# A static scheduler's clock, its arena's choice of holes, and the priority of staging subtractions, in a one-core transformer step

## The chip, the core and the metric

The kernel runs on one core of one Trainium2 chip. The metric is the device time of one execution in microseconds; before the change three runs took 2660.2, 2662.82 and 2666.45 us, median 2662.82. A core has five engines that each work off a queue of their own in order and meet at semaphores: TensorE (PE, matmuls and transposes into PSUM), VectorE (DVE), ScalarE (ACT), GpSimd (POOL), and SyncE (SP), which here issues the DMAs.

## The reference

One step of an encoder with two layers over 512 prompt and 32 sample tokens, D = 1024, all in float32. Layer 0 mixes tokens with a chunkwise retention, layer 1 with a differential attention against keys and values projected once after layer 0.

```python
def run_trunk(x, c, pos, ...):
    for l in range(2):
        mod = (silu(c) @ w_ada[l] + b_ada[l]).reshape(b, 9, D)
        h = modulate(x, g_norm[l, 0], mod[:, 0], mod[:, 1])        # rms_norm * (1 + scale) + shift
        x = x + 0.5 * mod[:, 2] * rms_norm(swiglu(h, w_ffn_in[l, 0], w_ffn_out[l, 0]), g_norm[l, 1])
        h = modulate(x, g_norm[l, 2], mod[:, 3], mod[:, 4])
        y = retention_mixer(h, ...) if l == 0 else diff_mixer(h, k, v, k_past, v_past, ...)
        x = x + mod[:, 5] * rms_norm(y, g_norm[l, 3])
        h = modulate(x, g_norm[l, 4], mod[:, 6], mod[:, 7])
        x = x + 0.5 * mod[:, 8] * rms_norm(swiglu(h, w_ffn_in[l, 1], w_ffn_out[l, 1]), g_norm[l, 5])
        if l == 0:
            k, v = shared_kv(x, c, ...)
    return x, new_ret, k, v

def diff_attention(q, k, v, lam):          # per head: two softmaxes, o = (p1 - lam * p2) @ v
    p = softmax(where(visible, q @ k.T * DH**-0.5, -inf))
    return (p[:, :, 0] - lam * p[:, :, 1]) @ v
```

## The kernel before

**Layout.** Activations lie with features on the partitions and tokens in the free dimension. The 544 tokens are two halves: H0 has 256, H1 has 288 (256 prompt and the 32 sample tokens). Each half goes through the stages by itself, and the two are interleaved, so that one half's products cover the other's norms.

**Main products.** A weight matrix is cut into units of 128 output features with 8 (some 6) blocks of 128 inputs. Each float32 weight and each operand is split in two parts, a rounded one (fp32r) and what the rounding left, and a block costs three matmuls (hi x hi, hi x lo, lo x hi; L595). There are 17,280 of them, 8,640 for each half; I number them in their order on PE. A weight block comes by DMA into one of three buffers, ScalarE casts it into the high part of a tile `w` (L574), and VectorE subtracts that from the raw weights for the low part (L577): this is *staging*, 544 times, in `w_conv`. There are four `w` tiles, and PE may begin a unit only when both parts are there (`launch`).

**Boundaries.** At the end of a stage, half by half: square the outputs and add them up (L803, L806 on ScalarE, L808 on VectorE), sum over the partitions by matmul (L700), mean and eps (L704), the power -1/2 on GpSimd (L706), broadcast by matmul (L711), scale and add to X (L845, L849); then the same for the norm ahead of the next stage (a second L808, L700, L704, L706, L711), and its operands (L738 on VectorE, L747 on ScalarE, L753 on VectorE). So a half passes L700 and L711 twice at a boundary, and VectorE works between for a chain of 23 rows or more.

**Attention** (`at_head`, `at_block`, `at_sample`). Per head and half two blocks of 128 queries: logits (L1513), mask, maximum, exponentials, the mix of the two softmaxes (L1522 to L1542), transposes (L1548), the product with v (L1555), a norm (L1570 to L1576), transposes (L1584). The 32 sample tokens go in four passes of two heads each (L1622 to L1690). The second half's sixteen blocks and four passes must all be through before the first unit of the output projection (`w_out_b`) of that half, which begins at product 15,048.

**What sets the order.** The whole program is unrolled by a scheduler, `Sched`, that runs when the kernel is built: generators stand for processes, each step names an engine, a cost in ns, a function that records the instructions, and a priority (lower goes first). The scheduler keeps a clock. When an engine is free by that clock, it takes the ready step of the lowest priority number and records it. What comes out is a fixed order on each engine; on the chip every engine keeps to it. The order of main products by unit is fixed beforehand (`plan`, from the path `_path`); where everything else stands among them is what the clock decides. The costs of steps:

```python
def c_r(n):                       # one matmul of a main product with n columns
    return max(256, n) / 2.4 + 3
def c_dve(n):
    return (64 + n) / 0.96
```

**Memory.** Operands lie in tiles `SLOT`, taken in pairs (high and low part); all else of varying size (outputs Y, scores, heads' keys and values, tables) comes from one `Arena`, whose requests wait until a hole is large enough: those of 600 numbers and more take the first hole from the low end, smaller ones the first from the high end. A head of the second half takes 1504 numbers, a block up to 1424, the sample passes 2992 together.

Of the kernel before, what the change touches and what calls it, by code (L numbers as in the profile page):

```python
# [50 lines left out]
def _path():  # L51
# [3 lines left out]
    for e in ((0, 1), (0, 2), "kv", (1, 0)):  # L55
# [10 lines left out]
       0, Q, 0), (F2, 10, Q, 0), (F2, 36, OB, 0), (F2, 47, OB, 0), (F2, 49, F2, 0), (F2, 68, F2, 0)]  # L66
NSLOT = (35, 34)
NW = 4
# [20 lines left out]
class Arena:  # L89
# [3 lines left out]

    def take(self, n):
        hs = self.holes
        for i in (range(len(hs)) if n >= 600 else range(len(hs) - 1, -1, -1)):
            o, m = hs[i]
            if m >= n:
                if m == n:
                    del hs[i]  # L100
                elif n >= 600:
                    hs[i] = (o + n, m - n)
                else:
                    hs[i] = (o, m - n)
                    o += m - n
                return (o, n)
        return None

# [133 lines left out]
def c_r(n):  # L242
    return max(256, n) / 2.4 + 3

# [77 lines left out]
def yoco_step(ctx: ExitStack, tc: tile.TileContext, I, O):  # L322
    nc = tc.nc
# [38 lines left out]
    def fa(r, n=None, o=0, p0=0, p1=P):  # L362
        n = r[1] - o if n is None else n
        return FA[p0:p1, r[0] + o:r[0] + o + n]
# [326 lines left out]
    def rstd(acc, H, dim, pr=0):  # L691

        nb, n = (3, 96) if H else (2, P)
# [3 lines left out]
        def sums():  # L697
            for j in range(nb):
                for g in range(0, n, 32):
# [5 lines left out]
                                                     ALU.mult, ALU.add), pr)  # L705
        yield ("POOL", 200 + 170 * nb, lambda: nc.gpsimd.tensor_tensor(  # L706
            fa(t, nb, 4, 0, n), fa(t, nb, 0, 0, n), NHALF[:n, :nb], ALU.pow), pr)
# [387 lines left out]
    def ret_head(h, oo):  # L1095
# [11 lines left out]
        def finish(b, H, c0, n):  # L1107

            blks = ((0, P), (P, P)) if n == 256 else ((0, n),)
            rows = blks[0][1]  # L1110
            nb = len(blks)
            og = yield from get(2 * n)
            tk = yield from get(256 * nb)
            m = yield from get(8)

            def sq():
                for i in range(nb):
# [4 lines left out]
                                                          ALU.mult, ALU.add))  # L1122
            yield ("POOL", 200 + 170 * nb, lambda: nc.gpsimd.tensor_tensor(
                fa(m, nb, 4, 0, rows), fa(m, nb, 2, 0, rows), NHALF[:rows, :nb], ALU.pow))
# [149 lines left out]
        o = yield from get(256)  # L1274
# [294 lines left out]
    def sub_ln(b, rows, o, m, t):  # L1569
# [3 lines left out]
                                                     ALU.mult, ALU.add))  # L1573
        yield ("POOL", 370, lambda: nc.gpsimd.tensor_tensor(fa(m, 1, 2, 0, rows), fa(m, 1, 1, 0, rows),
                                                            NHALF[:rows, :1], ALU.pow))
# [209 lines left out]
TANH = (1,)  # L1785
FIN_P = 25
CONV_P = 3
# [4 lines left out]
ADA_LEAD = -22  # L1792
ARENA_N = 20344
RETH = 9
# [115 lines left out]
```

## Time and profile before

| | |
|---|---|
| three runs, median | 2662.82 us (2660.2 to 2666.45) |
| the profiled execution, its own time | 2668.01 us |
| its span, first to last instruction | 2666.2 us |
| mean granted TensorE clock | 0.977 |
| main products L595, busy | 2279.6 us, x17280 |
| staging casts L574 (ScalarE), busy | 556.8 us, x544, 1023 ns mean |
| staging subtractions L577 (VectorE), busy | 649.1 us, x544, 1195 ns mean |
| DMA | 400.57 MB, mean 150 GB/s |
| attention logits L1513, busy | 43.7 us, x128 |

Busy times are unions of an engine's intervals. Matmuls are pipelined: a matmul's own duration (292 ns mean for L595) is longer than the distance from one to the next, so a rate is read from how many there are in a stretch without waits. PEclk is the share of full clock that PE was granted; it takes the values 1.00 and 0.50 in the records, and a mean between them is a mix in time. A wait is idle time of an engine before an instruction, put down to what released it.

### The profile page before, as it was taken

The page shows a single profiled execution, that of the slowest core. Times are in us where ns is not written, and L with a number is a line of the kernel's source. Part 1 is how long each engine was busy: PE and PEld are TensorE (multiplying, and loading weights), DVE is VectorE, ACT ScalarE, POOL GpSimd, SP SyncE. Part 2 cuts the span into 40 slices and gives each one's busy share as a digit, 9 for nine tenths or more (in the row PEclk, how much of TensorE's full clock was granted, in tenths as well). Part 3 has the DMA queues.
Part 4 walks back from the last instruction along what each step waited for, and adds up shares of the span by engine and source line. Part 5 has one row for each costly group of instructions (what it writes and reads, how often), then busy time and mean ns, then how long its engine had stood idle before and what let it go on. Part 6 is the DMA issues. An engine that isn't in the chain of part 4 may idle for free. (4 is left out here: it accounts for less than half of the span.)

```text
span 2666.2 us, 48255 instructions
## 1 busy us (share of the span) xinstructions
PE 2558.3 (96%) x19908; PEld 2409.8 (90%) x19908; DVE 1402.8 (53%) x2716; ACT 1040.3 (39%) x2055; POOL 65.3 (2%) x88
## 2 busy tenths in 40 slices
PE   7999999999999999999999999999997999789998
PEld 5899998899999987999997999998897898479997
DVE  5223337754334474223359644557867766457555
ACT  3222224443323343222234424445654544344433
POOL 0000000000000000000000000000100000000000
PEclk9999999999999999999999999999998999789999
DMA  8722325732222258223238735556643454235553
GB/s 332 261 88 88 96 86 171 249 119 93 79 95 75 79 200 306 88 88 96 88 92 306 222 101 155 176 169 235 229 162 109 135 195 155 72 119 165 167 166 106
DMA packets 119549, 400.57 MB, mean 150 GB/s; under 512 B 13344, under 2 KB 31904, under 8 KB 109088
## 3 DMA queue, kind: packets, MB, share of 16 engines
q1 hardware_dynamic: 119328, 397.48, 45.0%
q8 instruction: 156, 2.56, 0.4%
q14 instruction: 65, 0.53, 0.1%
HBM read 384.19 MB, written 13.24 MB: 149 GB/s over the span
## 5 line engine op out<-in xcount | busy, mean ns | idle before, releaser
L595 PE MATMUL ps<-r,w 128*128 128x288 f32 (+1 forms) x17280 | 2279.6, 292 | 22.8 <-DVE w L577 18.2
L595 PEld LDWEIGHTS ps<-r,w 128*128 128x128 f32 x17280 | 2215.1, 192 | 86.3 <-issue 50.6
L577 DVE TENSOR_TENSOR w<-FA,w 128x1024 fp32r<-128x1024 f32 (+1 forms) x544 | 649.1, 1195 | 601.0 <-ACT w L574 599.3
L574 ACT CAST w<-FA 128x1024 fp32r<-128x1024 f32 (+1 forms) x544 | 556.8, 1023 | 958.1 <-PE ps L595 866.6
L931 DVE TENSOR_TENSOR FA<-ps,FA 128x256 f32<-128x256 f32 (+1 forms) x88 | 38.7, 441 | 186.1 <-PE ps L595 181.5
L895 ACT CAST r<-FA 128x256 fp32r<-128x256 f32 (+1 forms) x176 | 73.2, 417 | 129.5 <-DVE FA L931 92.4
L884 DVE TENSOR_TENSOR FA<-ps,FA 128x288 f32<-128x288 f32 (+1 forms) x144 | 63.2, 440 | 103.3 <-PE ps L595 101.2
L747 ACT ACTIVATE r<-FA,MOD 128x256 fp32r<-128x256 f32 (+1 forms) x168 | 63.5, 437 | 73.2 <-DVE FA L738 72.7
L896 DVE TENSOR_TENSOR r<-FA,r 128x256 fp32r<-128x256 f32 (+1 forms) x176 | 76.8, 437 | 23.2 <-ACT r L895 23.2
L501 PE MATMUL ps<-FA,SC 128*32 128x512 f32 x576 | 77.8, 619 | 6.5 <-DMA FA<-in_ada 6.5
L808 DVE TENSOR_TENSOR FA<-FA 128x256 f32<-128x256 f32 (+1 forms) x168 | 73.3, 437 | 13.3 <-ACT FA L806 12.1
L706 POOL TENSOR_TENSOR FA<-FA,NHALF 128x2 f32<-128x2 f32 (+1 forms) x24 | 27.6, 1151 | 1818.9 <-DVE FA L704 1321.2
L928 DVE SCALAR_TENSOR_TENSOR FA<-ps,FA 128x256 f32<-128x256 f32 (+1 forms) x88 | 38.6, 440 | 55.8 <-PE ps L595 55.8
L738 DVE SCALAR_TENSOR_TENSOR FA<-X,DRV,ps 128x256 f32<-128x256 f32 (+1 forms) x168 | 57.7, 397 | 17.2 <-PE ps L711 14.4
L753 DVE SCALAR_TENSOR_TENSOR r<-FA,MOD,r 128x256 fp32r<-128x256 f32 (+1 forms) x168 | 59.0, 402 | 8.9 <-ACT r L747 8.8
L919 ACT ACTIVATE FA<-ps 128x256 f32<-128x256 f32 (+1 forms) x88 | 34.5, 394 | 70.3 <-PE ps L595 70.2
L990 DVE TENSOR_TENSOR FA<-ps,FA 64x256 f32<-64x256 f32 (+1 forms) x128 | 56.1, 438 | 2.0
L986 DVE TENSOR_TENSOR FA<-ps,FA 128x256 f32<-128x256 f32 (+1 forms) x64 | 28.0, 438 | 51.5 <-PE ps L595 51.3
L845 DVE SCALAR_TENSOR_TENSOR FA<-FA,DRV,ps 128x256 f32<-128x256 f32 (+1 forms) x144 | 50.0, 398 | 5.8 <-PE ps L711 5.6
L882 ACT COPY FA<-ps 128x288 f32<-128x288 f32 (+1 forms) x96 | 36.5, 381 | 40.0 <-PE ps L595 40.0
L806 ACT ACTIVATE FA<-FA 128x256 f32<-128x256 f32 (+1 forms) x84 | 35.7, 428 | 31.7 <-DVE FA L884 31.2
L1513 PE MATMUL ps<-FA 128*128 128x128 f32 (+3 forms) x128 | 43.7, 469 | 1.7 <-ACT FA L1496 0.9
(145 smaller groups left out, 1134.1 us busy)
## 6 DMA issues: line engine op xcount, KB each, us to landing
FA<-in_w_ffn_in SPq DMA_DIRECT2D x256, 512.0 KB, 3.3
FA<-in_ada SPq DMA_DIRECT2D x80, 1024.0 KB, 6.7
FA<-in_w_ffn_out SPq DMA_DIRECT2D x95, 512.0 KB, 3.5
FA<-in_w_in_a SPq DMA_DIRECT2D x60, 512.0 KB, 3.3
FA<-in_w_ffn_out SPq DMA_DIRECT2D x61, 384.0 KB, 3.2
FA<-in_w_kv SPq DMA_DIRECT2D x22, 512.0 KB, 5.2
FA<-in_w_out_a SPq DMA_DIRECT2D x19, 512.0 KB, 3.4
FA<-in_w_q_b SPq DMA_DIRECT2D x16, 512.0 KB, 4.3
```

The costliest lines, as they stand in the source:

```text
L501: te.matmul(PS[b][32 * g:32 * g + 32, :], lhsT=SC[:, k, :], rhs=fa(ada_buf[u, k], 512, g * 512), start=(k == 0), stop=(k == 7))
L574: yield act(n, lambda: nc.scalar.copy(hi, src))
L577: yield dve(n, lambda: nc.vector.tensor_tensor(lo, src, hi.bitcast(F32), ALU.subtract))
L595: te.matmul(PS[b][:, :n], lhsT=w[:, a, k, :], rhs=x, start=(k == 0 and j == 0), stop=(k == u.nk - 1 and j == 2))
L738: nc.vector.scalar_tensor_tensor(fa(z, c1 - c0, o), X[:, f, c0:c1], DRV[:, gi, f, s:s + 1], PS[Rb][:, o:o + c1 - c0], ALU.mult, ALU.mult)
L747: nc.scalar.activation(op.hi(H, c0, c1), fa(z, c1 - c0, o), AF.Identity, bias=MOD[:, mi, f, s:s + 1])
L753: nc.vector.scalar_tensor_tensor(op.lo(H, c0, c1), fa(z, c1 - c0, o), MOD[:, mi, f, s:s + 1], op.hi(H, c0, c1).bitcast(F32), ALU.add, ALU. ...
L808: yield dve(n, lambda: nc.vector.tensor_tensor(acc, acc, fa(t), ALU.add))
L884: yield dvp(n, lambda: nc.vector.tensor_tensor(Y[:, f, c], PS[b][:, :n], Y[:, f, c], ALU.add), 15)
L895: yield act(n, lambda: nc.scalar.copy(op.hi(H), src), pr)
L896: yield dve(n, lambda: nc.vector.tensor_tensor(op.lo(H), src, op.hi(H).bitcast(F32), ALU.subtract), pr)
L990: nc.vector.tensor_tensor(fa(t1, n, n, x, x + 64), PS[b][y:y + 64, :n], fa(rr, n, NTOK + c.start, y, y + 64), ALU.mult)
```

## The change

The diff adds two lines near the top, so that line numbers of the changed kernel are higher by two (L595 becomes L597).

```diff
-NSLOT = (35, 34)
+NSLOT = (34, 34)
...
     def take(self, n):
+
         hs = self.holes
-        for i in (range(len(hs)) if n >= 600 else range(len(hs) - 1, -1, -1)):
-            o, m = hs[i]
-            if m >= n:
-                if m == n:
-                    del hs[i]
-                elif n >= 600:
-                    hs[i] = (o + n, m - n)
-                else:
-                    hs[i] = (o, m - n)
-                    o += m - n
-                return (o, n)
-        return None
+        fit = [(m, i) for i, (o, m) in enumerate(hs) if m >= n]
+        if not fit:
+            return None
+        m, i = min(fit)
+        o = hs[i][0]
...
 def c_r(n):
-    return max(256, n) / 2.4 + 3
+    return max(256, n) / 2.4 + 13.3
...
-        yield ("POOL", 200 + 170 * nb, lambda: nc.gpsimd.tensor_tensor(
+        yield ("POOL", 380 + 160 * nb, lambda: nc.gpsimd.tensor_tensor(
             fa(t, nb, 4, 0, n), fa(t, nb, 0, 0, n), NHALF[:n, :nb], ALU.pow), pr)
...
-        yield ("POOL", 370, lambda: nc.gpsimd.tensor_tensor(fa(m, 1, 2, 0, rows), fa(m, 1, 1, 0, rows),
+        yield ("POOL", 540, lambda: nc.gpsimd.tensor_tensor(fa(m, 1, 2, 0, rows), fa(m, 1, 1, 0, rows),
...
-FIN_P = 25
+FIN_P = 0
...
-ARENA_N = 20344
+ARENA_N = 20600
```

`c_r` is the cost by which the scheduler's clock counts a main product's matmul: 109.7 ns becomes 120.0 for 256 columns, 123.0 becomes 133.3 for 288. The `POOL` costs are those of the powers. `FIN_P` is the priority of the staging subtraction among VectorE's ready steps; the norm chain has priorities from 0 to 2, evictions 15 to 20. The arena takes the smallest hole that fits. One tile of `SLOT` goes (256 numbers per partition), and the arena gets 256. No instruction is added or taken away on the compute engines; they are recorded in another order.

The order on PE, at the end of the second half's attention, before the change. The first row is main product 15,084, the others stand directly behind it; `ps_...` are PSUM banks, FA is the arena:

```order
L595 MATMUL ps_150<-r_28_136,w_144 128x288
L1555 MATMUL ps_152<-FA 128x128 x3
L1548 MATMUL ps_154<-CT,FA 128x128 x4
L1555 MATMUL ps_154<-FA 128x128 x4
L1584 MATMUL ps_153<-CT,FA 128x128 x2
L1513 MATMUL ps_152<-FA 128x384
L1513 MATMUL ps_154<-FA 128x384
L1622 MATMUL ps_153<-FA 64x512 x2
L1548 MATMUL ps_152<-CT,FA 128x128 x3
L1555 MATMUL ps_152<-FA 128x128 x3
```

Twenty-four rows of this kind follow each other there without a main product between them, and twenty-one more behind product 15,102. The order after, behind main product 14,864, with the same kinds of rows (L1550 is L1548 before, L1586 is L1584, L1664 is L1662, L1557 is L1555, L1515 is L1513):

```order
L597 MATMUL ps_148<-r_24_97,w_144 128x256
L597 MATMUL ps_148<-r_26_99,w_144 128x256
L597 MATMUL ps_148<-r_27_100,w_144 128x256
L597 MATMUL ps_148<-r_26_99,w_144 128x256
L1550 MATMUL ps_153<-CT,FA 128x128 x3
L597 MATMUL ps_148<-r_2_75,w_144 128x256
L597 MATMUL ps_148<-r_3_76,w_144 128x256
L597 MATMUL ps_148<-r_2_75,w_144 128x256
```

The pieces of attention stand earlier and have main products between them: the last of them now stands behind product 14,928, before behind 15,102. The first L1622 of the sample passes stands behind product 14,214 (L1624), before behind 14,421.

The order on VectorE, at the boundary between attention and the last FFN for the first half, before the change: the operands of the next stage (L738, L753) and three staging subtractions (L577) behind them:

```order
L738 SCALAR_TENSOR_TENSOR FA<-X,DRV,ps_153 128x256 x4
L753 SCALAR_TENSOR_TENSOR r_16_89<-FA,MOD,r_15_88 128x256
L753 SCALAR_TENSOR_TENSOR r_18_91<-FA,MOD,r_17_90 128x256
L753 SCALAR_TENSOR_TENSOR r_0_73<-FA,MOD,r_28_101 128x256
L753 SCALAR_TENSOR_TENSOR r_2_75<-FA,MOD,r_1_74 128x256
L738 SCALAR_TENSOR_TENSOR FA<-X,DRV,ps_153 128x256
L884 TENSOR_TENSOR FA<-ps_147,FA 128x288
L577 TENSOR_TENSOR w_144<-FA,w_144 128x768
L753 SCALAR_TENSOR_TENSOR r_4_77<-FA,MOD,r_3_76 128x256
L577 TENSOR_TENSOR w_142<-FA,w_142 128x768
L577 TENSOR_TENSOR w_143<-FA,w_143 128x768
```

After the change the first two of these three subtractions (the 388th and the 389th of the program, now L579) stand in the first part of the same boundary, between the rows of the norm (L847, L851, L810 are L845, L849, L808 before), ahead of its second sum of squares:

```order
L579 TENSOR_TENSOR w_144<-FA,w_144 128x768
L810 TENSOR_TENSOR FA<-FA 128x256
L847 SCALAR_TENSOR_TENSOR FA<-FA,DRV,ps_152 128x256 x2
L851 TENSOR_TENSOR X<-X,FA 128x256 x2
L847 SCALAR_TENSOR_TENSOR FA<-FA,DRV,ps_152 128x256
L810 TENSOR_TENSOR FA<-FA 128x256
L851 TENSOR_TENSOR X<-X,FA 128x256
L579 TENSOR_TENSOR w_142<-FA,w_142 128x768
L810 TENSOR_TENSOR FA<-FA 128x256
L918 SCALAR_TENSOR_TENSOR FA<-FA,ps_147 128x288
```

The subtractions moved from behind the operands to between the norm's rows. The same holds at the other boundaries: between a half's two rows L700 there stand more subtractions on VectorE, and on PE more main products of the other half. Behind which main product these pairs of L700 rows stand:

| boundary (the half that ends) | before: first, second | after: first, second | subtractions between, before and after |
|---|---|---|---|
| layer 0, FFN to retention, H0 | 3042, 3114 | 3042, 3147 | 1, 6 |
| same, H1 | 3198, 3264 | 3219, 3333 | 1, 5 |
| retention to second FFN, H0 | 6132, 6192 | 6132, 6240 | 1, 5 |
| second FFN to keys and values, H0 | 9276, 9336 | 9276, 9381 | 1, 6 |
| same, H1 | 9432, 9516 | 9459, 9561 | 2, 3 |
| layer 1, FFN to attention, H0 | 12573, 12651 | 12573, 12678 | 3, 5 |
| attention to second FFN, H0 | 13509, 13584 | 13509, 13602 | 1, 4 |
| layer 1, FFN to attention, H1 | 13752, 13824 | 13752, 13899 | 2, 7 |
| attention to second FFN, H1 | 15312, 15384 | 15312, 15459 | 2, 7 |

The products that cover the chain are those between the first L711, which stands 6 to 18 products behind the first L700, and the second L700.

More of the change, by code (lines that the diff above doesn't have):

```diff
@@ L95, in take @@
         hs = self.holes
-        for i in (range(len(hs)) if n >= 600 else range(len(hs) - 1, -1, -1)):
-            o, m = hs[i]
-            if m >= n:
-                if m == n:
-                    del hs[i]
-                elif n >= 600:
-                    hs[i] = (o + n, m - n)
-                else:
-                    hs[i] = (o, m - n)
-                    o += m - n
-                return (o, n)
-        return None
+        fit = [(m, i) for i, (o, m) in enumerate(hs) if m >= n]
[3 more added lines that the diff above has]
+        o = hs[i][0]
+        if m == n:
+            del hs[i]
+        elif n >= 600:
+            hs[i] = (o + n, m - n)
+        else:
+            hs[i] = (o, m - n)
+            o += m - n
+        return (o, n)
     def put(self, r):
@@ L1122, in finish @@
                                                           ALU.mult, ALU.add))
-            yield ("POOL", 200 + 170 * nb, lambda: nc.gpsimd.tensor_tensor(
+            yield ("POOL", 380 + 160 * nb, lambda: nc.gpsimd.tensor_tensor(
                 fa(m, nb, 4, 0, rows), fa(m, nb, 2, 0, rows), NHALF[:rows, :nb], ALU.pow))
```

## The prediction

> **What bounds the kernel now.** I read the page first, then TensorE's waits, then the busy time stretch by stretch.
>
> ```profile
> span 2666.2 us, 48255 instructions
> PE 2558.3 (96%) x19908; PEld 2409.8 (90%) x19908; DVE 1402.8 (53%) x2716; ACT 1040.3 (39%) x2055; POOL 65.3 (2%) x88
> PE   7999999999999999999999999999997999789998
> PEclk9999999999999999999999999999998999789999
> ```
>
> TensorE is the bound: 96% busy, VectorE 53%, ScalarE 39%. Two things are left to win: the 108 us in which PE is idle (2666.2 - 2558.3), and the time at a lower clock, which the slices put into the last quarter. Who is waited for:
>
> ```profile
> PE ps L700 <- DVE FA L808: 27.9, 8, 11.7
> PE ps L595 <- DVE w L577: 18.2, 9, 5.2
> PE ps L1548 <- DVE FA L1542: 10.9, 6, 3.0
> PE ps L711 <- POOL FA L706: 10.8, 7, 3.2
> PE ps L501 <- DMA FA<-in_ada: 6.5, 8, 1.7
> ```
>
> Columns are the total in us, the number of waits and the longest. L700, L711 and L577 belong to the boundaries between stages (the norm of one half, and the staged weights); L1548 is attention. The first 11.7 us of L700 are the load of x at the start, and stay. Now the stretches in which this happens, behind one steady stretch:
>
> ```profile
> core 0: us, PE busy (x) PEld busy (x) DVE busy (x) ACT busy (x) POOL busy (x), PEclk, DMA share, GB/s
> 133.30:200.00 66.70, 66.70 (x531) 66.70 (x530) 17.66 (x21) 19.11 (x33) 0.00 (x0) 1.00 0.29 88
> 450.00:510.00 60.00, 52.34 (x421) 39.66 (x420) 51.59 (x131) 29.58 (x67) 3.92 (x4) 0.94 0.74 271
> 964.00:1006.00 42.00, 38.89 (x332) 28.35 (x331) 34.44 (x87) 17.09 (x35) 2.44 (x3) 0.96 0.80 296
> 1396.00:1444.00 48.00, 41.67 (x343) 31.35 (x342) 43.56 (x108) 22.92 (x47) 3.34 (x2) 0.93 0.76 278
> 1998.00:2080.00 82.00, 63.32 (x462) 61.62 (x461) 63.39 (x148) 36.55 (x74) 6.01 (x3) 0.83 0.33 108
> 2265.00:2349.40 84.40, 59.74 (x272) 39.46 (x272) 30.42 (x87) 28.11 (x90) 5.98 (x10) 0.70 0.19 64
> 2382.00:2416.00 34.00, 23.16 (x158) 22.24 (x157) 26.37 (x69) 15.05 (x34) 3.17 (x1) 0.75 0.26 84
> ```
>
> In the steady stretch PE never waits and 531 matmuls take 66.70 us: 125.6 ns each. Elsewhere I count as lost what is not busy at full clock, length minus busy times PEclk. The five boundary stretches: 60.0 - 52.34 x 0.94 = 10.8; 42.0 - 37.3 = 4.7; 48.0 - 38.8 = 9.2; 82.0 - 52.6 = 29.4; 34.0 - 17.4 = 16.6. Together **71 us**, of which 47 are idle time (lengths less busy: 7.7 + 3.1 + 6.3 + 18.7 + 10.8) and 24 the clock. The end of attention, 2265 to 2349: 84.4 - 59.74 x 0.70 = **42.6 us**. These two pools, 114 us, are what an order can win; the rest is products.
>
> **The change part by part.** *The length of a main product.* The scheduler counted 109.7 ns for 256 columns and 123.0 for 288, mean 116.3; now 120.0 and 133.3, mean 126.7. The trace says 125.6, so its clock ran 7% fast on the engine that bounds, and now runs right. Nothing is added; rows move. In the order of before PE reaches product 15,084 (of 17,280) with eight of the sixteen attention blocks of the second half and two of its four sample passes not through, and has no main product that may run. That is the 84.4 us stretch. In the order after, the first row of the sample passes stands at product 14,214 instead of 14,421 and the last attention row at 14,928 instead of 15,102, with main products between the pieces; the first product that needs attention's output stands at 15,048. So 120 products, 15 us, are to spare. The whole 42.6 us can go, if the pieces stay hidden in the new place. What they meet there: blocks follow each other more closely, with 18 to 48 products between a block's logits and its transpose where the first three heads of before have 27 to 39. The nearest row for that density:
>
> ```profile
> 2072.00:2265.00 193.00, 191.19 (x1461) 175.30 (x1461) 127.59 (x237) 93.05 (x196) 6.00 (x10) 0.99 0.52 167
> ```
>
> By line, in the same stretch, the transposes:
>
> ```profile
> L1548 PE MATMUL ps<-CT,FA 128*128 128x128 f32 x31 | 4.9, 273 | 0.0
> ```
>
> It holds ten blocks and two passes and lost 193 - 191.19 x 0.99 = 3.7 us; the transposes waited 0.0. VectorE is 66% busy; the end of attention brings 30.4 us of its work. So the new waits cost between 0 and all of the 42.6; I take 8, near the row. **Term: -35 us, bounds -42.6 and, with all of it waiting anew, 0; a loss is rival 3.**
>
> *The subtractions first on VectorE.* They take L577's place in the row of ready work from priority 25 to 0. The group, and from the timeline two of its three long waits:
>
> ```profile
> L577 DVE TENSOR_TENSOR w<-FA,w 128x1024 fp32r<-128x1024 f32 (+1 forms) x544 | 649.1, 1195 | 601.0 <-ACT w L574 599.3
> ```
>
> ```profile
> 2016.43 4.93 PE L595 MATMUL ps<-r,w 128*128 128x288 f32 x19 [4.28 <-DVE w L577]
> 2410.67 1.65 PE L595 MATMUL ps<-r,w 128*128 128x256 f32 x6 [5.23 <-DVE w L577]
> ```
>
> In the rows of before that stand with the change three subtractions come behind the norm's rows, so PE runs out of staged weights at a unit's end, waits, and only then finds the sums of squares. In the order after they stand between the norm's rows. Of the 18.2 us I count 17 as gone. The price: the chain between a half's two sums of squares gets longer. I count it in the order for nine of the ten (the tenth is woven with its neighbour): subtractions within, 14 before and 48 after, so 34 x 1.195 = 40.6 us more of VectorE; main products of the other half that PE has meanwhile, 534 before and 903 after, so 369 x 125.6 ns = 46.3 us more. The cover grows with the chain: the waits at L700, 14.6 us without start and end, fall by some 6. Without that cover the 40.6 us would stand on the path.
>
> The wait at L711 is for the power on GpSimd. It takes 0.85 us alone, and 3.14 where subtractions follow it:
>
> ```profile
> 2054.17 3.14 POOL L706 TENSOR_TENSOR FA<-FA,NHALF 96x3 f32<-96x3 f32 x1 [14.32 <-DVE FA L704]
> 2054.24 2.36 DVE L577 TENSOR_TENSOR w<-FA,w 128x1024 fp32r<-128x1024 f32 x2
> 2376.27 0.85 POOL L706 TENSOR_TENSOR FA<-FA,NHALF 96x3 f32<-96x3 f32 x1 [31.10 <-DVE FA L704]
> ```
>
> The second power of a half has a subtraction among the next three rows of VectorE in eight places of ten before, in one after; and in seven of nine places 12 to 21 main products now stand between it and L711. Of its 10.8 us (1.3 at the end, which stays) I count 6 as gone. What comes late next is the first product of the new stage: at the second and third stage of layer 0 the other half has 6 and 0 products left between L711 and it, so I add 3. Idle time: -17 - 6 - 6 + 3 = -26.
>
> The clock. Two waits around 460 and 488, then PE's clock behind the two waits of the timeline above and behind 453:
>
> ```profile
> PE ps L700 <- DVE FA L808: 2.0, 1, 2.0
> PE ps L595 <- DVE w L577: 1.3, 1, 1.3
> ```
>
> ```profile
> 2014.90:2021.70 6.80, 5.27 (x22) 5.27 (x23) 4.07 (x7) 1.34 (x4) 0.00 (x0) 0.50 0.56 167
> 2407.40:2414.20 6.80, 3.53 (x16) 3.53 (x17) 5.82 (x11) 1.31 (x5) 0.00 (x0) 0.50 0.33 91
> 453.00:460.00 7.00, 4.90 (x54) 3.27 (x42) 6.96 (x19) 3.21 (x7) 0.69 (x1) 1.00 0.87 338
> ```
>
> Behind the waits of 4.28 and 5.23 us PE has 6.8 us at 0.50; behind two of 1.3 us by 460 the clock stays 1.00; the one of 2.0 us, near 488, stands in the stretch whose clock is 0.94. So waits of about 2 us decide. The waits left at L700 average 1 us, and I leave 3 or 4 half-clock stretches at 2.5 us (6.8 x 0.75 busy x 0.5): of the 24 us, 14 go. **Term: -40 us, bounds -68 (the 71 less 3, half of L501's waits for DMA; the rest of them lie at the start) and 0** (a loss would need the 40.6 us uncovered, against 46.3 of cover).
>
> [...]
>
> *The rest.* The table of r0 tiles goes from 35 to 34, but tiles are taken in pairs, 17 either way; the arena's 256 numbers more and the powers' new costs (540, 700, 860 ns) leave PE's order nearly as it is; the smallest hole that fits moves attention's rows by some tens of products. I put these at 0, within the bounds of the first term. Start (until 76 us) and end (the last chain of norms, no product left) have the same rows.
>
> The sum, against the profiled execution: 2666.2 us of span and 1.8 around it are 2668.0; less 35 and 40 is 2593. The median of the three runs, 2662.8, lies 5.2 below the profiled one, so 2588; with one term or the other mostly rounded against me, **2590**.
>
> **The rivals.**
>
> 1. *The boundaries give nothing back*: the longer chain costs what the waits gain, since VectorE is already 77% to 91% busy in the boundary stretches, and powers meet more subtractions. For it: the 3.14 us row. Against it: the 46.3 us of cover, and the rows behind the second power. Time: 2663 - 35 = 2628. [...]
>
> 2. *Attention wins nothing*: its chain of VectorE, ScalarE and PE is as long as before and PE waits in its new place, in smaller pieces. For it: the 18-product distances. Against: the 193 us stretch. Time: 2663 - 40 = 2623.
>
> 3. *Slower*: PE takes its queue in order, and the attention rows stand earlier in it; a row whose input is late now holds back main products that before would have run. Sixteen transposes of blocks, eight of heads and four in each of the four sample passes are 40 rows. At 2 us each and 2.5 for the clock behind it that is 180 us, less 42.6 and 40: 2663 + 97 = 2760. It decides when the rows wait 2.1 us on average, clock included (83 / 40). Against it: in the 193 us stretch the transposes of ten blocks waited 0.0.
>
> 4. *The change doesn't move the time*: what waits in the order only changes its name. 2663. Against it: TensorE's products in the starved stretch are a few dozen, and there are main products to fill it.
>
> **How the numbers follow.** Forecast 0.64 at 2590; rival 1, 0.13 at 2628; rival 2, 0.13 at 2623; rival 3, 0.06; rival 4, 0.04. The full pools would give 2663 - 111 = 2552; the range goes from 2562, most of both, to 2634, beyond either rival alone, and leaves out rivals 3 and 4 and the tails. Faster by over 0.2% (5 us, about what a measurement of this kernel tells from none) 0.90, within it 0.04, slower 0.06.
>
> **What would show it.** Right, if the stretch at half clock before L595's product 15,084 is gone and PE's busy share there is 9 in every slice; if the waits of L595 for L577 are under 3 us in all; if waits at L700 stay, shorter than 2 us each; if the powers of L706 stay under 1.5 us. Wrong, if L1548 and L1584 (two lines lower in the changed kernel) wait for VectorE in many pieces before product 14,928, or if the mean clock stays at 0.977.

## The result, and the profile after

Four runs of the changed kernel took 2593.27 to 2600.41 us, median **2597.54**, beside 2660.2 to 2666.45, median 2663.73, of the kernel before. The ratio is 0.9751, 95% interval 0.9733 to 0.9769. The forecast was 2590, its range 2562 to 2634.

The page of the changed kernel (profiled at 2600.41 us, mean clock 0.993):

```profile
span 2598.6 us, 48242 instructions
PE 2528.3 (97%) x19908; PEld 2386.6 (92%) x19908; DVE 1399.2 (54%) x2716; ACT 1039.1 (40%) x2055; POOL 56.7 (2%) x88
PE   7999999999999999999999999999999999999997
PEclk9999999999999999999999999999999999999999
L708 POOL TENSOR_TENSOR FA<-FA,NHALF 128x2 f32<-128x2 f32 (+1 forms) x24 | 19.7, 819 | 1844.2 <-DVE FA L706 784.6
```

The dips of PE and of its clock in the last quarter are gone: 9 in every slice but the first and the last. The same instructions as before stand on every compute engine (19908, 2716, 2055, 88). A power takes 819 ns on average. Whom TensorE waits for (total in us, times, longest):

```profile
PE ps L702 <- DVE FA L810: 17.3, 7, 11.7
PE ps L503 <- DMA FA<-in_ada: 13.3, 17, 2.0
PE ps L597 <- ACT r L749: 5.2, 2, 2.6
PE ps L1081 <- DVE FA L996: 4.8, 12, 0.6
PE ps L597 <- DVE FA L918: 3.1, 2, 1.8
PE ps L597 <- DVE FA L886: 2.8, 1, 2.8
PE ps L597 <- ACT FA L808: 2.7, 2, 1.4
PE ps L713 <- POOL FA L708: 1.7, 2, 1.2
PE ps L597 <- DVE w L579: 0.4, 1, 0.4
```

Waits for staged weights fell from 18.2 to 0.4 us, for powers from 10.8 to 1.7, for sums of squares from 27.9 to 17.3, of which the load of x is 11.7. No transpose of attention (L1550, L1586) is left in the list. In their place stand waits of main products for L918, L886 and L808 (L916, L884 and L806 before): the first product of a unit has to wait for a PSUM bank that an eviction has not yet emptied. L808 itself empties no bank, it squares X; but each of these products, and the one that waits 2.6 us for L749 at 2355 us, begins 0.15 us behind the end of an eviction on VectorE (L918, L886 or L930). So I count all six as waits for evictions: 3.1 + 2.8 + 2.7 + 2.6 = 11.2 us. One of those put down to L808:

```profile
2334.96 0.41 DVE L918 SCALAR_TENSOR_TENSOR FA<-FA,ps 128x256 f32<-128x256 f32 x1
2335.03 0.44 ACT L808 ACTIVATE FA<-X 128x288 f32<-128x288 f32 x1
2335.52 0.71 PE L597 MATMUL ps<-r,w 128*128 128x256 f32 x4 [1.36 <-ACT FA L808]
```

L1081 (L1079 before, 0.3 us) is new too, and L503, the product that makes the modulation vectors and waits for its weights' DMA, doubled from 6.5.

To place the time I cut both kernels at the same main products. The windows below begin and end where products 3024, 3420, 6120 and 6700, then 13,488, 14,060, 15,300 and 15,700 begin: the boundary from the first FFN to retention, the retention, the boundary from retention to the FFN, the boundary ahead of attention (first half), attention of the second half, and the boundary behind it. Columns as in the prediction's table of windows. Before:

```profile
core 0: us, PE busy (x) PEld busy (x) DVE busy (x) ACT busy (x) POOL busy (x), PEclk, DMA share, GB/s
438.55:521.75 83.20, 75.25 (x608) 62.14 (x607) 71.67 (x176) 39.40 (x82) 4.62 (x5) 0.96 0.70 251
521.75:954.81 433.06, 433.06 (x3192) 408.94 (x3191) 189.19 (x381) 157.06 (x365) 15.25 (x23) 1.00 0.29 93
954.81:1064.42 109.61, 105.51 (x850) 83.75 (x849) 66.00 (x162) 41.99 (x84) 3.14 (x4) 0.98 0.78 283
1988.59:2094.09 105.50, 86.82 (x663) 84.94 (x661) 78.53 (x173) 48.50 (x93) 6.70 (x4) 0.87 0.38 120
2094.09:2373.88 279.79, 253.84 (x1758) 217.46 (x1757) 158.11 (x324) 128.06 (x298) 11.98 (x20) 0.91 0.42 136
2373.88:2441.28 67.40, 56.56 (x451) 55.49 (x450) 50.96 (x115) 31.98 (x63) 4.03 (x2) 0.87 0.41 125
```

After, with three short windows behind single waits at the end:

```profile
core 0: us, PE busy (x) PEld busy (x) DVE busy (x) ACT busy (x) POOL busy (x), PEclk, DMA share, GB/s
438.85:508.91 70.06, 67.80 (x575) 58.69 (x573) 63.05 (x159) 36.27 (x78) 3.95 (x5) 1.00 0.68 245
508.91:952.63 443.72, 438.33 (x3210) 410.06 (x3209) 199.19 (x398) 160.59 (x370) 15.11 (x23) 1.00 0.28 94
952.63:1071.79 119.16, 110.64 (x867) 86.51 (x866) 66.29 (x162) 42.05 (x84) 3.22 (x4) 0.96 0.76 277
1994.70:2081.94 87.24, 80.00 (x662) 78.42 (x661) 76.59 (x172) 48.06 (x93) 3.18 (x4) 0.96 0.45 146
2081.94:2316.91 234.97, 232.91 (x1759) 204.71 (x1757) 156.54 (x325) 126.74 (x299) 11.78 (x20) 1.00 0.48 162
2316.91:2373.14 56.23, 52.30 (x450) 51.47 (x449) 49.03 (x114) 31.87 (x63) 1.70 (x2) 0.97 0.46 150
2012.00:2018.80 6.80, 6.80 (x53) 6.62 (x54) 4.11 (x11) 2.38 (x6) 0.79 (x1) 0.75 0.21 58
1019.40:1026.20 6.80, 6.78 (x39) 4.91 (x40) 1.98 (x3) 1.35 (x2) 0.00 (x0) 0.75 0.65 250
2056.00:2062.80 6.80, 6.47 (x67) 6.18 (x67) 6.38 (x15) 3.09 (x8) 0.85 (x1) 1.00 0.40 146
```

The three late stretches win 18.3, 44.8 and 11.2 us, the first 13.1; the retention and the boundary behind it lose 10.7 and 9.6. In part that is work that moved across a cut (the first has 33 PE rows fewer, the next two 18 and 17 more), so I count lost time: the length minus PE's busy time, of which what lies in an interval at half clock counts half. The prediction took a stretch's busy time times its mean clock instead, which goes astray where idle time is spread unevenly over full and half clock: in its 84.4 us at the end of attention 45.5 us are lost, not 42.6. The first clock record is at 28.3 us in the kernel before and at 17.0 after; ahead of it I count half clock in both, since 32 products of L472 (L474) take 1.91 us there and 1.08 us later.

| lost time, us | before | after | difference |
|---|---|---|---|
| five boundary stretches (products 3024 to 3420, 6120 to 6700, 9264 to 9700, 13,488 to 14,060, 15,300 to 15,700) | 72.9 | 34.5 | -38.4 |
| attention, 14,060 to 15,300 | 46.8 | 2.1 | -44.7 |
| everything else | 27.3 | 35.5 | +8.2 |
| PE busy, counted at full clock, up to the last main product | 2504.5 | 2511.4 | +6.9 |
| behind the last main product | 14.8 | 15.2 | +0.4 |
| span | 2666.2 | 2598.6 | -67.6 |

The +8.2 are 5.4 in the retention (L1081), 1.5 between products 12,552 and 13,080, 1.2 at product 9822 (L1301 waits for L740) and 0.1 in all the rest.

### The profile page after: what moved, and what is told of

The parts are those of the page before. It is cut to its first block, busy times and chain, and to the rows that moved or that the text cites. A ratio compares the mean times of both kernels' runs of the same rounds, so it can differ in the third digit from the quotient of the medians.

```text
span 2598.6 us, 48242 instructions
## 1 busy us (share of the span) xinstructions
PE 2528.3 (97%) x19908; PEld 2386.6 (92%) x19908; DVE 1399.2 (54%) x2716; ACT 1039.1 (40%) x2055; POOL 56.7 (2%) x88
## 4 chain that ended last, share of the span: by engine, by line
PE 79%; issue 9%; DVE 6%; DMA 5%; ACT 1%; SPq 0%; POOL 0%; POOLq 0%; DVEq 0%; ACTq 0%
PE ps L597 69%; DMA FA<-in_ada 4%; PE ps L503 2%; DVE w L579 2%; PE ps L1515 1%; ACT w L576 1%; PE ps L1557 1%; DVE FA L740 1%; PE ps L1188 1%; PE ps L1200 1%; DVE FA L992 1%; DVE r L755 0%; DMA X<-in_xb 0%; PE ps L713 0%; PE ps L1550 0%
## 5 line engine op out<-in xcount | busy, mean ns | idle before, releaser
L597 PE MATMUL ps<-r,w 128*128 128x288 f32 (+1 forms) x17280 | 2276.8, 291 | 16.8 <-ACT r L749 5.2
L597 PEld LDWEIGHTS ps<-r,w 128*128 128x128 f32 x17280 | 2205.7, 191 | 86.6 <-issue 53.9
L579 DVE TENSOR_TENSOR w<-FA,w 128x1024 fp32r<-128x1024 f32 (+1 forms) x544 | 649.0, 1194 | 586.8 <-ACT w L576 580.1
L886 DVE TENSOR_TENSOR FA<-ps,FA 128x288 f32<-128x288 f32 (+1 forms) x144 | 62.5, 438 | 100.9 <-PE ps L597 99.6
L503 PE MATMUL ps<-FA,SC 128*32 128x512 f32 x576 | 76.4, 610 | 13.5 <-DMA FA<-in_ada 13.3
L749 ACT ACTIVATE r<-FA,MOD 128x256 fp32r<-128x256 f32 (+1 forms) x168 | 63.9, 437 | 46.7 <-DVE FA L740 46.2
L810 DVE TENSOR_TENSOR FA<-FA 128x256 f32<-128x256 f32 (+1 forms) x168 | 72.7, 435 | 14.2 <-ACT FA L808 13.0
L930 DVE SCALAR_TENSOR_TENSOR FA<-ps,FA 128x256 f32<-128x256 f32 (+1 forms) x88 | 38.3, 438 | 48.8 <-PE ps L597 48.6
L740 DVE SCALAR_TENSOR_TENSOR FA<-X,DRV,ps 128x256 f32<-128x256 f32 (+1 forms) x168 | 58.3, 396 | 9.7 <-PE ps L713 9.4
L921 ACT ACTIVATE FA<-ps 128x256 f32<-128x256 f32 (+1 forms) x88 | 34.5, 394 | 70.5 <-PE ps L597 70.4
L755 DVE SCALAR_TENSOR_TENSOR r<-FA,MOD,r 128x256 fp32r<-128x256 f32 (+1 forms) x168 | 59.1, 399 | 1.8 <-ACT r L749 1.6
L708 POOL TENSOR_TENSOR FA<-FA,NHALF 128x2 f32<-128x2 f32 (+1 forms) x24 | 19.7, 819 | 1844.2 <-DVE FA L706 784.6
L992 DVE TENSOR_TENSOR FA<-ps,FA 64x288 f32<-64x288 f32 (+1 forms) x128 | 56.1, 438 | 2.0
L847 DVE SCALAR_TENSOR_TENSOR FA<-FA,DRV,ps 128x256 f32<-128x256 f32 (+1 forms) x144 | 50.4, 396 | 6.6 <-PE ps L713 6.6
L884 ACT COPY FA<-ps 128x288 f32<-128x288 f32 (+1 forms) x96 | 36.3, 380 | 43.2 <-PE ps L597 43.2
L808 ACT ACTIVATE FA<-FA 128x256 f32<-128x256 f32 (+1 forms) x84 | 35.0, 427 | 27.4 <-DVE FA L886 24.9
L808 ACT ACTIVATE FA<-X 128x256 f32<-128x256 f32 (+1 forms) x84 | 34.1, 425 | 25.1 <-DVE X L851 23.0
```

The lines of the kernel that those rows point to most:

```text
L503: te.matmul(PS[b][32 * g:32 * g + 32, :], lhsT=SC[:, k, :], rhs=fa(ada_buf[u, k], 512, g * 512), start=(k == 0), stop=(k == 7))
L579: yield dve(n, lambda: nc.vector.tensor_tensor(lo, src, hi.bitcast(F32), ALU.subtract))
L597: te.matmul(PS[b][:, :n], lhsT=w[:, a, k, :], rhs=x, start=(k == 0 and j == 0), stop=(k == u.nk - 1 and j == 2))
L740: nc.vector.scalar_tensor_tensor(fa(z, c1 - c0, o), X[:, f, c0:c1], DRV[:, gi, f, s:s + 1], PS[Rb][:, o:o + c1 - c0], ALU.mult, ALU.mult)
L749: nc.scalar.activation(op.hi(H, c0, c1), fa(z, c1 - c0, o), AF.Identity, bias=MOD[:, mi, f, s:s + 1])
L808: yield act(n, lambda: nc.scalar.activation(fa(t), src[:, f, c], AF.Square))
```

## Experiments

The kernel before ran beside each batch: medians 2663.57, 2661.1 and 2664.08 us in the first, second and third. "Attention" is the window between products 14,060 and 15,300: 279.8 us before, 235.0 after.

### One part at a time: the priority, the clock

My theory was the prediction's: the priority of L579 wins the boundaries, the scheduler's clock, by `c_r`, wins attention, and the two are independent. ("Old" and "right" clock below mean `c_r` with 3 and with 13.3; the granted clock of PE is another thing.) The rival for attention was that memory decides. When the kernel is built, the scheduler can write down what it grants and when. The first sample pass asks for 2992 numbers of the arena behind product 14,184 in the kernel before, and behind 14,178 after:

```
                 holes when asked           granted behind product
before           544, 768, 904              14,388
after            256, 768, 3496             14,178 (at once)
after, FIN_P 25  544, 768, 768, 2440        14,373
after, old c_r   544, 768, 1160             14,397
```

Three heads are allowed at once (`ATH = 3`), and the pass needs heads 0 and 1, so a pass that waits for memory keeps their places. "After" has one hole that fits; the kernel with the old priority has the same total, cut in pieces. So the changed kernel could have won attention by the clock or by a hole.

**only_fin**, before with the priority alone:

```diff
-FIN_P = 25
+FIN_P = 0
```

> The kernel before with the subtractions' priority alone changed (25 to 0). Theory A (the priority makes the boundary term, the scheduler's clock the attention term): the boundaries move by the 23 us that the whole change moved them, attention's end stays starved: 2664 - 23 = 2641. Rival B (the priority alone lengthens the norm chains, and only the right clock covers them): 2664 or more.

Measured: 2643.66 us (2642.55 to 2647.61), ratio 0.993 (0.9915 to 0.9945), 20 us less. Attention stays at 277.0. TensorE's waits in this kernel:

```profile
PE ps L700 <- DVE FA L808: 14.7, 4, 11.5
PE ps L595 <- DVE FA L916: 9.3, 3, 4.4
PE ps L595 <- ACT FA L806: 5.0, 3, 1.8
PE ps L595 <- DVE FA L928: 3.9, 1, 3.9
PE ps L595 <- DVE FA L884: 3.2, 1, 3.2
```

The waits for staged weights are gone from the list's upper rows, and waits for evictions stand there instead: 9.3 + 5.0 + 3.9 + 3.2 = 21.4 us (behind L806 too an eviction on VectorE ends 0.15 us before the product each time).

**no_fin**, after with the old priority (`FIN_P = 25`).

> The changed kernel with the priority put back to 25. Theory A: attention's 45 us stay, the boundary's 23 go: 2598 + 23 = 2621. Theory H (attention's gain does not come from the right clock as such but from the moment at which the sample passes are granted their 2992 numbers of arena, behind product 14,178 in the changed kernel; here, with the same clock, it is behind 14,373, as late as before): part of attention's 45 us goes too, 2621 to 2660, and the stretch around product 15,084 shows PE waiting.

Measured: 2640.29 us (2639.1 to 2641.83), ratio 0.9915 (0.99 to 0.993). The waits for L579 are back (15.4 us) and those for powers too (10.2); a power takes 1379 ns on average here, 820 in only_fin. Its row for attention:

```profile
2107.90:2349.37 241.47, 237.60 (x1758) 206.71 (x1757) 157.96 (x324) 126.87 (x298) 11.57 (x20) 0.99 0.49 157
```

241.5 us, although the memory came late: the right clock wins 38 us of attention without the hole. This kernel also has the changed arena, tiles and costs of the powers; no run has the clock and nothing else.

**no_cr**, after with the old clock:

```diff
 def c_r(n):
-    return max(256, n) / 2.4 + 13.3
+    return max(256, n) / 2.4 + 3
```

> The changed kernel with the main product's cost put back (3 instead of 13.3). Theory A: the boundary gain stays, attention is starved as before: 2598 + 45 = 2643. If the arena's choice of holes or the 256 numbers were behind attention's gain: 2598.

Measured: 2643.44 us (2642.07 to 2647.45), ratio 0.9929 (0.9914 to 0.9944): what the priority alone gives.

```profile
2081.99:2359.01 277.02, 251.18 (x1757) 215.54 (x1757) 158.48 (x323) 128.08 (x298) 11.78 (x20) 0.92 0.42 135
```

Arena, tiles and the powers' costs, which this kernel has, do nothing without the clock.

**nocr_early**, no_cr in which the sample passes ask for their memory as soon as the half's first head is loaded:

```diff
+        if p == 0:
+            yield hds[0].ld
+            at["smem"] = yield from get(1056 + 1024 + 576 + 64 + 16 + 2 * P, -2)
         for hd in hds:
             yield hd.ld
         yield ("get", at["ssem"], 1, p)
-        if p == 0:
-            at["smem"] = yield from get(1056 + 1024 + 576 + 64 + 16 + 2 * P, -2)
```

> As the run without the main product's new cost, and the sample passes ask for their 2992 numbers when the first head of the second half is loaded, not the second; they get them behind product 14,178 at the latest. Theory A (the clock is what counts): 2643, the stretch before product 15,084 stays starved. Theory H (the grant is what counts): 2600, the stretch is gone with the old, fast clock; the last attention row stands behind product 15,009.

Measured: 2595.1 us (2594.05 to 2597.8), ratio 0.9747 (0.9731 to 0.9763), as fast as the changed kernel, with the old clock.

```profile
2076.09:2307.62 231.53, 231.10 (x1758) 203.67 (x1757) 156.16 (x323) 127.65 (x298) 11.95 (x20) 1.00 0.49 162
```

0.4 us of attention are lost. **before_early** (third batch) does the same to the kernel before, with nothing else.

> The kernel before, and only the sample passes' request is made when the first head of the second half is loaded. Theory H (the moment of the grant): most of attention's 45 us is won by this alone, with the old clock and the old priority, less what the pieces lose that still stand behind product 15,000 (the last behind 15,102): 2662 - 35 = 2627, attention's stretch 240 to 250 us instead of 280. Theory A (the grant helps only together with the other edits): 2655 or more.

Measured: 2626.08 us (2625.2 to 2630.99), ratio 0.986 (0.9845 to 0.9874).

```profile
2097.56:2337.55 239.99, 233.94 (x1758) 205.30 (x1757) 156.54 (x324) 126.45 (x298) 11.67 (x20) 0.99 0.48 158
```

So the moment of the grant is enough by itself for 40 of the 45 us, and the clock, with the arena's edits beside it, for 38; without both, attention starves. What the rows of PE show, counted in the traces (rows of attention that stand behind one main product, without another between):

```
               clock  memory   first L1622  last attention  PE rows behind    attention,
                               (L1624)      row behind      15,084 / 15,102   us
before         old    late     14,421       15,102          122 / 118         279.8
only_fin       old    late     14,442       15,102          122 / 118         277.0
no_fin         right  late     14,406       15,102           18 / 21          241.5
before_early   old    early    14,226       15,102            0 / 1           240.0
nocr_early     old    early    14,205       15,009            0 / 0           231.5
after          right  early    14,214       14,928            0 / 0           235.0
```

With the right clock the scheduler gives a piece of attention fewer main products for the same time, so even a late start ends nearly in time.

### What the changed kernel still loses

The next four start from the changed kernel with the early request, which by itself leaves the order of PE as it is there.

**dma300**: the modulation weights come in pieces of 1 MB, and L503 waits for them. The theory: the scheduler counts DMA too fast, and L503 stands too early on PE.

```diff
 def c_dma(n):
-    return max(475, n / 360)
+    return max(475, n / 300)
```

> The changed kernel with the early request (its order is that of the changed kernel), and the scheduler's cost of a DMA byte raised (bytes/300 ns instead of bytes/360; the fullest slice of the profile moved 332 GB/s). Theory D (with the product's length right, the DMA's cost is now the clock that runs fast, so the modulation products L503 stand too early and their waits for in_ada doubled, 6.5 to 13.3 us): these waits fall to 5 us or less, time 2597 - 8 = 2589. Rival (the transfers pace PE wherever the rows stand): waits stay or pass to staging, 2597.

Measured: 2595.43 us (2593.23 to 2597.81), ratio 0.9751 (0.973 to 0.9772).

```profile
PE ps L503 <- DMA FA<-in_ada: 3.9, 4, 1.7
```

The waits fell from 13.3 to 3.9 us; lost time fell by 1.7 (70.4 us instead of 72.1). The boundary at 6120 lost 8.0 us instead of 13.3, but attention 5.1 instead of 2.1 and the boundary at 9264 4.8 instead of 3.1; the other stretches differ by 1.4 us at most, some up and some down. The theory was right on the wait and wrong on the time.

**lat200**: the retention's L1081 transposes what L996 has just written, and waits 0.6 us at most, twelve times. The theory: the scheduler's delay from VectorE to PE, 80 ns, is too short.

```diff
-    TO_PE = {"PE": 130, "ACT": 80, "DVE": 80, "POOL": 200, "DMA": 0}
+    TO_PE = {"PE": 130, "ACT": 80, "DVE": 200, "POOL": 200, "DMA": 0}
```

> The changed kernel with the early request, and VectorE's latency to PE counted as 200 ns instead of 80. Theory L (the new waits of the key transposes L1081 for VectorE, 4.8 us in 12 pieces of up to 0.6, come from this number, which the fast clock had covered): they fall below 1.5 us, time 2597 - 4 = 2593. Rival (they hang on the order on VectorE): they stay, 2597.

Measured: 2596.86 us (2592.31 to 2601.16), ratio 0.9759 (0.9738 to 0.978), and 4.7 us of L1081 are left of 4.8. The theory falls. What stands ahead of L996 on VectorE was not tried.

**bnd02**: at the boundary from retention to the FFN, the prediction's place with 0 products of cover, `BND` says how the halves are interleaved; here it gets the numbers of the boundary before it.

```diff
-BND = {(0, 1): (7, 7, 7, 12), (0, 2): (6, 7, 5, 4), 'kv': (7, 8, 6, 7), (1, 0): (1, 4, 4, 6)}
+BND = {(0, 1): (7, 7, 7, 12), (0, 2): (7, 7, 7, 12), 'kv': (7, 8, 6, 7), (1, 0): (1, 4, 4, 6)}
```

> The changed kernel with the early request, and twelve units of the other half instead of four before the boundary from retention to the second FFN (the path's numbers 7, 7, 7, 12). Theory C (that boundary lost 10 us since the longer norm chain has no main product left to cover it): the two waits of L702 there (2.9 us) and the half clock behind them go, time 2597 - 6 = 2591. Rival (the modulation's DMAs set the pace there): 2597.

Measured: 2593.96 us (2590.45 to 2595.02), ratio 0.9746 (0.9728 to 0.9765).

```profile
954.91:1052.17 97.26, 93.63 (x758) 79.51 (x757) 69.06 (x154) 45.23 (x86) 3.78 (x3) 1.00 0.68 241
```

The stretch loses 3.6 us (97.26 - 93.63) instead of 13.3. It has 109 PE rows fewer, which its neighbours have instead, so I take the three stretches from product 3420 to 9264 together: 880.9 us instead of 885.5, and 11.5 lost instead of 18.6. Not all of it is the norm's cover: L503 waits 5.4 us for DMA at that boundary in the changed kernel, 1.7 here and 2.6 in the next stretch; L702 waits 2.9 and 0.4. By the whole time this kernel isn't separated from the changed one.

**evict**: the waits for evictions. The theory: they come from L579 standing ahead of the evictions on VectorE. The rival: evictions that go first only push the norm back.

```diff
-        go(u.post(H, b), 20)
+        go(u.post(H, b), -1)
...
-                    yield act(n, lambda: nc.scalar.copy(Y[:, f, c], PS[b][:, :n]), 15)
+                    yield act(n, lambda: nc.scalar.copy(Y[:, f, c], PS[b][:, :n]), -1)
...
-                    yield dvp(n, lambda: nc.vector.tensor_tensor(Y[:, f, c], PS[b][:, :n], Y[:, f, c], ALU.add), 15)
+                    yield dvp(n, lambda: nc.vector.tensor_tensor(Y[:, f, c], PS[b][:, :n], Y[:, f, c], ALU.add), -1)
```

> The changed kernel with the early request, and the evictions of main products ahead of the subtractions (priority -1 instead of 15 to 20). Theory E (what took the place of the staging waits are main products that wait for a bank whose eviction stands behind subtractions and the norm, 8.6 us of L597 for L918, L886 and L808): these go, time 2597 - 8 = 2589. Rival (the norm chain then comes later and has no cover: its second sums stand at the first product of the new stage, 3168, 6240, 9408): 2600 to 2615.

Measured: 2607.23 us (2604.78 to 2608.42), ratio 0.9797 (0.9779 to 0.9815), 10 us more than after. The waits for evictions are gone (the stretch from product 13,488 to 13,730 is idle 0.5 us instead of 4.6), and the sums of squares are late, in this kernel's waits:

```profile
PE ps L702 <- DVE FA L810: 24.3, 10, 11.6
PE ps L597 <- DVE w L579: 3.5, 4, 1.3
```

The first boundary, 442.95 to 526.18 us there, takes 83.2 us again, as before the change, at a granted clock of 0.92. The rival held.

How an eviction comes to be late, in the changed kernel: VectorE ahead of the bank that PE waits for (start, length, instruction):

```profile
2006.41 0.95 DVE L579 TENSOR_TENSOR w<-FA,w 128x768 fp32r<-128x768 f32 x1
2007.28 0.42 DVE L810 TENSOR_TENSOR FA<-FA 128x256 f32<-128x256 f32 x1
...
2010.13 0.95 DVE L579 TENSOR_TENSOR w<-FA,w 128x768 fp32r<-128x768 f32 x1
2011.00 0.42 DVE L810 TENSOR_TENSOR FA<-FA 128x256 f32<-128x256 f32 x1
2011.34 0.45 DVE L918 SCALAR_TENSOR_TENSOR FA<-FA,ps 128x288 f32<-128x288 f32 x1
```

and PE in the same time:

```profile
2004.82 5.31 PE L597 MATMUL ps<-r,w 128*128 128x288 f32 x39
2011.93 1.03 PE L597 MATMUL ps<-r,w 128*128 128x288 f32 x6 [1.80 <-DVE FA L918]
```

VectorE is never idle there, from 2003.5 to 2013.2 us: the norm's rows (priorities 0 to 2) and the subtractions, with the evictions behind. In that place the priority only said which product waits: with the evictions first their waits went, and those at L702 rose from 17.3 to 24.3 us.

### Is the right clock worth anything with the early request?

**nocr_bnd** (old clock, early request, the `BND` of bnd02), **cr8_bnd** (the same with `+ 8` in `c_r`) and **d330_bnd** (13.3, `BND`, early request, and `n / 330` in `c_dma`):

> The changed kernel with the old cost of a main product (3), the early request and the wider cover before the second FFN. If the right clock is worth nothing here: as the earlier run with the old cost, 2595, less the 4 us of the cover: 2591. If the right clock is worth its gains at the late boundaries (about 12 us) more than its losses in the retention (about 7): 2597 or more.

> As that, with 8 instead of 3 for a main product's cost, between the old and the new. If the clock's two effects (late boundaries better, retention's waits worse) grow evenly, the time lies between the two neighbours, 2591 to 2594; if the order is simply drawn anew with each value, it can lie anywhere within 10 us of them.

> The changed kernel with the early request, the wider cover before the second FFN, and a DMA byte at bytes/330 ns. If the modulation's waits at that boundary (11.4 us in all with the cover alone) are a loss of their own: they fall below 6, time 2594 - 5 = 2589. If they only stand where PE would wait anyway: 2594.

| | median us | range | ratio | interval |
|---|---|---|---|---|
| nocr_bnd (+3) | 2593.85 | 2590.0 to 2594.89 | 0.9732 | 0.9718 to 0.9747 |
| cr8_bnd (+8) | 2599.13 | 2596.1 to 2606.28 | 0.9759 | 0.974 to 0.9778 |
| bnd02 (+13.3, second batch) | 2593.96 | 2590.45 to 2595.02 | 0.9746 | 0.9728 to 0.9765 |
| d330_bnd (+13.3) | **2591.82** | 2588.53 to 2593.86 | 0.973 | 0.9714 to 0.9746 |

The old and the right clock give the same time. Their profiles differ: nocr_bnd loses 76.9 us and bnd02 64.6, but PE is busy 2501.4 us in the one and 2513.0 in the other, at full clock. The clock between them gives no time between in the medians, though its interval overlaps theirs. My reading is that each number draws the whole order anew and the parts scatter (from product 12,552 to 13,080 cr8_bnd loses 6.9 us, nocr_bnd 2.6; the profile of cr8_bnd is that of its slowest run, 2606.28 us); more numbers were not tried. In d330_bnd the waits of L503 are 5.8 us, in bnd02 11.4. It has the lowest median, 5.7 us under the changed kernel; their intervals overlap, and from nocr_bnd it isn't separated at all.

## Why the prediction was right, and where it wasn't

**The boundaries, -40: right, in part by errors against each other.** The five stretches lost 38.4 us less: idle time fell by 22.9 (26 was said) and the rest, 15.5, is the clock (14 was said). The signs came as named: L579 0.4 us (under 3 was said); L702's waits, the start's 11.7 left out, no longer than 1.6 us (under 2 was said); the powers 819 ns on average (under 1.5 us was said). But these three kinds of wait fell by 17.8, 10.6 and 9.1 us, together 37.5 where 29 were said, and what came in their place was larger too. "What comes late next" was put at 3 us for the first products of new stages in layer 0. Those wait 0.9 us (for L755, behind product 9578); evictions, which I hadn't looked at, wait 11.2 in layer 1: the longer chain of VectorE holds back not only the norm but the banks. L503's waits for DMA grew by 4.3 us in the five stretches and weren't in the sum.

The boundary from retention to the FFN, with 0 products of cover, is the only one that got worse (5.8 to 13.3 us lost). The longer chain alone doesn't do it: only_fin and no_cr have the same rows L700 there, behind 6132 and 6240, and lose 6.2 and 6.9 us with the old clock. L503 waits 1.6 and 1.7 us for DMA there in those two, 5.4 in the changed kernel, and 5.7 in no_fin, which has the new clock and the old chain. So the loss there goes with the new clock more than with the longer chain, and the prediction had the clock act on attention alone.

**Attention, -35: the sign and the place right, the size too small, the cause only half.** The measured -44.7 lies beyond the term's bound of -42.6. The pool was read 3 us too small (45.5 in the 84.4 us, 46.8 in all), and the 8 us kept back for new waits were not needed: 2.1 us are lost there. The rows moved as said and stayed hidden. That the clock moved them was half of it. The clock, with the arena's edits and the powers' costs, gives 38 us (no_fin against before), the early memory alone 40 (before_early) or, beside the new priority, 45 (nocr_early against no_cr). In the changed kernel both are there, since the new order leaves a hole of 3496 numbers at the moment of the request. The prediction put the smallest hole that fits at "some tens of products" and the arena's size at nothing. no_cr has both and starves, so neither is enough; whether the changed kernel would have found that hole without them wasn't run.

**The rest, 0: wrong by 15 us.** The sum -75 of the two terms came out at -83.1 (38.4 + 44.7). Outside the pools 8.2 us more are lost, and PE is busy 6.9 us longer at full clock with the same 19908 matmuls. That the time came within 8 us of the forecast is these errors against each other, 8 too little in the terms and 15 left out. For the first I had left the steady stretches out of the sum: a new order is new there too, and the retention, which lost nothing before, got its waits for L996 with the new clock (no_fin has them, 5.5 us; only_fin and no_cr lose 0.1 us in that stretch). For the 6.9 us I have no cause. They come with the clock (nocr_early is busy 2502.1 us by the same count, less than before; no_fin 2514.0) and are spread over many stretches; whether small matmuls among main products cost more than in a row was not measured.

**The rivals.** Rival 1 (boundaries give nothing) and rival 2 (attention gives nothing) fall with only_fin and no_fin: the parts give 20 and 23 us by themselves. The parts add up to 43 us and the whole is 66. no_fin shows part of why: by its profile it wins 38 us in attention and loses 12 elsewhere. With the new clock and the old priority the waits at L702 are 26.0 us, those for L579 15.4 and for powers 10.2, little less than in the kernel before, while L503 (12.1) and L1081 (5.5) wait 11 us more. The priority takes away 15.0 of L579's, 8.7 of L702's and 8.5 of the powers', and attention's other 6.5 us (241.5 to 235.0), and so is worth 43 us beside the right clock (2640.3 - 2597.5). Without it, it is worth 20: only_fin then waits 21.4 us for evictions, the changed kernel 11.2. Rival 3 (forty rows of attention wait 2 us each) needed waits that the trace doesn't have: 2.1 us in the whole stretch. Rival 4 falls with the result.

**The clock after short waits.** The wait of 1.80 us shown above is followed by a window at 0.75, one of 1.97 us at 1017 by another, and one of 1.37 us at 2055 by a window at 1.00. "Waits of about 2 us decide", as the prediction had it, doesn't hold: in the kernel before a wait of 1.69 us at 460.9 cost no clock (1.00 from 460.9 to 470.0 us) and one of 1.68 at 969.1 did (0.50 from 970.4 to 973.8). The last section has more of the clock's records.

## What to carry to other kernels

Where a kernel's order is made by a scheduler at build time, ask of a starved stretch first what its work waited for in the scheduler, memory above all: one request asked for earlier was worth as much here as the clock's calibration. A higher priority for one step on an engine that was full in that place turned its wait into the next one's here (only_fin: 18.2 us for staged weights before, 21.4 for evictions after), so look beforehand at which buffers the pushed-back steps hold. And since any number of such a scheduler redraws the whole order, charge a change for the steady stretches too, and test it beside one or two neighbours before crediting its reason.

## What the hardware showed beyond that

Half clock came after waits of 1.80 and 1.97 us, for 3.41 us each. In the clock's records of the changed kernel it holds for 3.41 us from 1020.5, 2013.8, 2027.5 and 2355.1 us, and for 6.83 us from 976.1, behind two waits of 1.47 and 1.46 us close together at 972. In the kernel before seven of the nine intervals at the boundaries held for 6.83 or 10.24 us, the longest wait ahead of each being 2.0 to 5.2 us. I had counted 6.8 us for every stretch of half clock that is left; of the five between the start and the end of the changed kernel four take 3.41.

The length of a wait alone doesn't tell these cases apart. In the records of the two kernels, before and after, the changes between full and half clock lie whole multiples of 3.41 us from each other, to 4 ns. I cut these two traces at that spacing, in step with the changes, from 40 us to the last main product, and took PE's busy share in each piece at full clock: 17 pieces were busy under 0.50, and all 17 were followed by one at half clock; of six from 0.50 to 0.56, three were; of the other 1,446, none. The wait of 1.80 us lies inside one piece (2010.4 to 2013.8 us, busy 0.55); the one of 1.37 at 2055 leaves its piece 0.60 busy. In the kernel before the one of 1.69 at 460.9 leaves its piece (458.4 to 461.8) 0.50 busy, and the one of 1.68 at 969.1 its own (967.0 to 970.4) 0.40, with another of 0.38 us behind it. These are counts of two executions; what sets the clock wasn't shown.
